# An encoder layer on one core: first loads of w_ff2 held behind a square, operands laid on or 64 bytes beside 128-byte multiples

## The chip, the cores and the metric

The kernel runs on one NeuronCore of a Trainium2 chip. The metric is the device time of one execution in microseconds. The kernel before took 1215.16 us, the median of 3 runs (1214.47, 1215.16 and 1220.26). The profile is of one further execution, which took 1215.97 us by the same clock.

Five engines are named as the profile names them: PE is TensorE's matmul, PEld its load of the stationary operand, DVE is VectorE, ACT is ScalarE, POOL is GpSimd, SP is SyncE. SP and POOL issue DMAs here.

## The reference

One encoder layer over 512 positions of 1024 channels, in float32:

```python
h = layer_norm(x, ln0_g, ln0_b)
proj = h @ w_in                       # q, k, v | z | x, B, C | dt | gates: 11328 columns
ya = neighbourhood_attention(q, k, v, rpb) @ w_attn_br
y  = ssd_chunked(silu(conv(x, B, C)), dt) in both directions, 8 groups
ys = rms_norm(y * silu(z)) @ w_ssd_br
h = layer_norm(ALPHA * h + (g0 * ya + g1 * ys) @ w_o)
out = layer_norm(ALPHA * h + square(relu(h @ w_ff1)) @ w_ff2)
```

`w_ff1` is 1024 x 4096 and `w_ff2` is 4096 x 1024.

## The kernel before, in words

**Three matmuls for one.** Each product is taken in float32r with operands split in a high and a low part. `mm3` (L351 to L354) issues three matmuls into one PSUM bank: stationary high with moving high (L352), stationary low with moving high (L353), stationary high with moving low (L354); the profile names a group as output, moving operand, stationary operand: in `ps_f<-wh_f,sqh` the weights move, in `ps_f<-h1Th,wh_f` they are stationary. Weights come from HBM as a float32 tile `ws_*` (1 MB, [128, 8, 256] or [128, 4, 512]), ACT copies it to the high part `wh_*`, and DVE or POOL subtracts to get the low part `wl_*`, each in two halves.

**Buffers.** The pool `wp` holds two buffers each of `ws`, `wh` and `wl`, 8192 bytes per partition. A matrix product therefore runs as a stream of "slabs": load, split, multiply, with the next slab's load waiting until a `ws` buffer is free. The pools `gc`, `sb`, `ge`, `rx0`, `fp`, `ffp` lie around `wp` in the order in which they are opened, from the left or from the right, so that the size of one shifts those behind it.

**Stages.** Up to about 512 us come the projections and the state-space branch, whose engine orders a planner class (`Plan`) writes out: group by group, `ps_x` (inputs x, B, C; 512 columns of `hT` moving, except group 0 with 256), `ps_z` (the slab `wh_z` is the moving operand, 256 columns, `hT` stationary), the scan, and `ps_sbr` (512 columns of `yT` moving). Then attention (to 716 us), its branch and gates, `ps_o` (256 columns of `wo` moving, `mgh`/`mgl` stationary), and the MLP from about 854 us.

**The MLP.** `ff1_tile(fq, f)` makes tile f (of 8) of quarter fq of the hidden layer: 24 matmuls of 512 columns into a bank `ps_f` (tag `mm`, two banks), then on ACT a Relu into `rl` (L1554), which frees the bank, and a Square into `r2` (L1560). The first four tiles of quarter 0 are taken in two halves of 256 columns, the first halves ahead of the second layer norm. Quarters 0 and 1 run first. Then `ff2_strassen` multiplies two quarters by `w_ff2` with seven block products. Its right operands are sums of two 512 x 512 blocks of `w_ff2`, made by DMA: `block` (L1448) loads one block of 1 MB from POOL's queue, and `plus` (L1454) adds the second in two DMAs of 512 KB that accumulate in SBUF. The tile is `w2r_*`: two of three lie in the pool `ffp` and one in `wp`'s `ws`. Its split writes `wh_f` on ACT (L1459) and `wl_f` on DVE (L1460). The left operands `sqh`, `sql` are tiles of tag `gt` in the pool `ge`, stationary.

**Order.** Past the planner's part the framework's scheduler sets each engine's order from the program and its dependencies; each engine and each DMA queue then runs strictly in that order. ACT therefore holds everything behind an instruction that waits.

Of the kernel before, what the change touches and what calls it, by code (L numbers as in the profile page):

```python
# [11 lines left out]
F32 = mybir.dt.float32  # L12
F32R = mybir.dt.float32r
# [6 lines left out]
P = 128  # L20
# [3 lines left out]
KD = D // P  # L24
# [9 lines left out]
OFF_Q, OFF_K, OFF_V, OFF_Z = 0, 1024, 2048, 3072  # L34
# [34 lines left out]
W0_ENG = lambda nc: (nc.gpsimd, nc.vector, nc.gpsimd, nc.vector)  # L69
# [3 lines left out]
class Plan:  # L73
# [16 lines left out]
                self.ap = self.make()  # L90
            return self.ap

    def tile(self, name, tag, pool, shape, dtype):
        return Plan.Tile(self, name, tag, lambda: pool.tile(shape, dtype, tag=tag, bufs=self.tags[tag],
                                                            name=name))

    def have(self, name, tag, ap):
        t = Plan.Tile(self, name, tag, None)
# [214 lines left out]
def encoder_layer(ctx, tc, x, w_in, w_attn_br, w_ssd_br, w_o, w_ff1, w_ff2, pcols, rows64,  # L313
                  d_skip, ln_rows, rpb_pad, consts, lmask, out, dbg=None):
    nc = tc.nc
# [6 lines left out]
    wp = ctx.enter_context(tc.tile_pool(name="wp", bufs=2))  # L322
# [20 lines left out]
                              op=ALU.subtract)  # L343
        return hi, lo

    def weights(parts, nk, ncol, name, eng=nc.vector, pool=None, after=None):
        hi = (pool or wp).tile([P, nk, ncol], F32R, tag="wh", name=f"wh_{name}")
        lo = (pool or wp).tile([P, nk, ncol], F32R, tag="wl", name=f"wl_{name}")
        return split_weights(parts, nk, ncol, name, hi, lo, eng, pool, after)

    def mm3(o, lh, ll, rh, rl, start, stop):  # L351
# [48 lines left out]
    gcp = gc.__enter__()  # L400
# [3 lines left out]
    gep = ge.__enter__()  # L404
# [2 lines left out]
    ident = cst[:, CC_ID : CC_ID + P]  # L407
    tri_f = cst[:, CC_TF : CC_TF + P]
    tri_b = cst[:, CC_TB : CC_TB + P]
    ones = gcp.tile([P, P], F32, name="ones")  # L410
    nc.vector.memset(ones, 1.0)
    eps = cp.tile([P, 1], F32, name="eps")
# [38 lines left out]
    def local(name, tag, shape, dtype=F32):  # L451
        return plan.tile(name, tag, sbp, shape, dtype)

    def slab(name, parts, nk, ncol, engs):

        ws = plan.tile(f"ws_{name}", "ws", wp, [P, nk, ncol], F32)
        wh = plan.tile(f"wh_{name}", "wh", wp, [P, nk, ncol], F32R)
        wl = plan.tile(f"wl_{name}", "wl", wp, [P, nk, ncol], F32R)
        c = 0
        keys = []  # L460
        for j, (src, r0, c0, n) in enumerate(parts):
            op("SP", 4.0 * n / ncol, lambda src=src, r0=r0, c0=c0, n=n, c=c: nc.sync.dma_start(
                ws()[:, :, c : c + n],
                src[r0 : r0 + nk * P, c0 : c0 + n].rearrange("(k p) c -> p k c", p=P)),
               r=[("behind", 0)], w=[(ws.name, j)], at=4.8 if name == "x0" else 4.4)
            keys.append((ws.name, j))
# [295 lines left out]

    def group_slabs(g):
        wb = slab(f"bc{g}", [(w_in, 0, OFF_B + g * P, P), (w_in, 0, OFF_C + g * P, P)], KD, 256,
                  (nc.gpsimd, nc.gpsimd) if g else W0_ENG(nc)[:2])
        wx = slab(f"x{g}", [(w_in, 0, OFF_X + g * 256, 256)], KD, 256,
                  (nc.gpsimd, nc.gpsimd) if g else W0_ENG(nc)[2:])
        return wb, wx

    def z_project(g):  # L770
        wh, wl = slab(f"z{g}", [(w_in, 0, OFF_Z + g * 256, 256)], KD, 256, (nc.gpsimd, nc.gpsimd))
        sz = local(f"sz{g}", "sz", [P, NT, 256])
        for c2 in range(2):
            ps = bank(f"ps_z{g}_{c2}", "mm", [P, 2, 256])
            for j in range(2):
                c = slice((2 * c2 + j) * P, (2 * c2 + j + 1) * P)
                for k in range(0, KD, 2):
                    def mms(k=k, j=j, c=c, ps=ps):
                        for q in (k, k + 1):
# [339 lines left out]
    for s in range(2):  # L1119
# [35 lines left out]
    for pr in range(NH // 2):  # L1155
# [25 lines left out]
        for hh in range(2):  # L1181
            h = 2 * pr + hh
# [91 lines left out]
    for k in range(KD):  # L1274
        ins = nc.scalar.activation(aTh[:, k], aT[:, k], AF.Copy)
# [95 lines left out]
    for t2 in range(2):  # L1371
        toks = (2 * t2, 2 * t2 + 1)
        for s in range(4):
            cs = slice(s * 256, (s + 1) * 256)
            wo = wos[s]
            tag = ("mm", "so")[s % 2]
            pss = {t: psx.tile([P, 256], F32, tag=tag, bufs=BANKS[tag], name=f"ps_o{t}_{s}")
                   for t in toks}
            for k in range(KD):
                for t in toks:  # L1380
                    ts_ = slice(t * P, (t + 1) * P)
                    mm3(pss[t], mgh[:, k, ts_], mgl[:, k, ts_], wo[0][:, k, :], wo[1][:, k, :],
                        k == 0, k == KD - 1)
            for t in toks:
                nc.vector.scalar_tensor_tensor(out=h0[t][:, cs], in0=h0[t][:, cs], scalar=ALPHA,
                                               in1=pss[t], op0=ALU.mult, op1=ALU.add)
        if t2:

            early = []
            for s in range(2):  # L1390
                w1 = weights([(w_ff1, 0, s * 256, 256)], KD, 256, f"f1_0_{s}")
                for j in range(2):
                    tag = ("so", "yd", "cb", "so")[2 * s + j]
                    ps = psx.tile([P, S], F32, tag=tag, bufs=BANKS[tag], name=f"ps_f1_0_{2 * s + j}")
                    ff1_half(w1, j, ps, 0)
                    early.append((w1, ps))
        for t in toks:
            layer_norm_core(epp, h0[t], acc[t], f"1_{t}")
        to_channels([acc[t] for t in toks], toks[0], 2, PC_G1, PC_B1, h1Th, h1Tl, epp, f"h1_{t2}")
# [5 lines left out]

    ffp = ctx.enter_context(tc.tile_pool(name="ffp", bufs=1, reuse_waits="tile"))
    NQ = D_FF // D
    pairs = [[gep.tile([P, 4, 256], F32R, tag="gt", bufs=4, name=f"sq{n}_{i}") for n in "hl"]
             for i in range(2)]
    turn = {"parts": 2, "raw": 0}  # L1410

    def parts(name, shape):

        turn["parts"] += 1
        if turn["parts"] % 3 == 0:
            return third(w3p, name, shape)
        return [wp.tile(shape, F32R, tag=n, name=f"{n}_{name}") for n in ("wh", "wl")]

    def raw(name):
        turn["raw"] += 1  # L1420
# [13 lines left out]
    def ff2_strassen(h, q0, r2):  # L1434
# [1 line left out]


        np_ = len(r2)
        begun, made = set(), [0]

        def rows(i, n, c, k=slice(0, 4)):
            r0 = q0 * D + (i * np_ + c) * 512
            return w_ff2[r0 : r0 + 512, n * 512 : (n + 1) * 512].rearrange(
                "(k p) c -> p k c", p=P)[:, k]

        def block(name, i, n, c):
            t = raw(f"{h}_{name}_{c}")
            nc.gpsimd.dma_start(t, rows(i, n, c))  # L1448
# [113 lines left out]
    slab = [None]  # L1562
# [5 lines left out]
    for fq in range(2):  # L1568
        for f in range(KD):
            ins = ff1_tile(fq, f, False)  # L1570
            if fq == 0 and f == 4:

                for t in range(NT):
                    for i, o in ((0, ALU.mult), (1, ALU.add)):
                        aff = nc.gpsimd.tensor_tensor(out=acc[t], in0=acc[t], in1=row1[i], op=o)
                        if t == 0 and i == 0:
                            tc.add_manual_dep(aff.ins, ins.ins.name, mybir.DependencyInfo(
                                mybir.DependencyClass.Sync, mybir.DependencyReason.DATA),
                                reason="behind the first channels")
# [107 lines left out]
```

## Time and profile before

| | us |
|---|---|
| median of 3 runs | 1215.16 |
| profiled execution, whole | 1215.97 |
| its span, first to last instruction | 1214.2 |
| PE busy | 1174.4 |
| DVE busy | 778.4 |
| ACT busy | 609.4 |
| POOL busy | 542.3 |

The span leaves out 1.8 us around the first and last instruction. PE's busy time is the union of its matmuls' times; a matmul's own duration in the profile runs from its issue to its modelled end and overlaps the next, so that what one matmul costs in a row of equal ones is the distance from its start to the next start, called its pace below. Where one stage has a long row of the same kind, the pace is read from the first and last start of one source line and its count.

### The profile page before, as it was taken

The page shows a single profiled execution, that of the slowest core. Times are in us where ns is not written, and L with a number is a line of the kernel's source. Part 1 is how long each engine was busy: PE and PEld are TensorE (multiplying, and loading weights), DVE is VectorE, ACT ScalarE, POOL GpSimd, SP SyncE. Part 2 cuts the span into 40 slices and gives each one's busy share as a digit, 9 for nine tenths or more (in the row PEclk, how much of TensorE's full clock was granted, in tenths as well). Part 3 has the DMA queues.
Part 4 walks back from the last instruction along what each step waited for, and adds up shares of the span by engine and source line. Part 5 has one row for each costly group of instructions (what it writes and reads, how often), then busy time and mean ns, then how long its engine had stood idle before and what let it go on. Part 6 is the DMA issues. An engine that isn't in the chain of part 4 may idle for free.

```text
span 1214.2 us, 16823 instructions
## 1 busy us (share of the span) xinstructions
PE 1174.4 (97%) x6306; PEld 1003.2 (83%) x6306; DVE 778.4 (64%) x1427; ACT 609.4 (50%) x1012; POOL 542.3 (45%) x588
## 2 busy tenths in 40 slices
PE   5999999999999999999999989999979999999996
PEld 5988798989888888788888878889968888878885
DVE  7748475665666665534888975356662467498856
ACT  4576573836355563324677873442254454365510
POOL 1158967777788767303666730014251131221000
PEclk9999999999999999999999999999999999999998
DMA  7144243333333342234432333353185586888511
GB/s 230 53 143 139 89 137 104 114 119 117 105 103 116 115 135 70 70 104 100 101 73 63 83 104 105 104 198 96 56 208 153 159 190 184 186 210 214 152 61 52
DMA packets 131169, 149.21 MB, mean 123 GB/s; under 512 B 22928, under 2 KB 105488, under 8 KB 131088
## 3 DMA queue, kind: packets, MB, share of 16 engines
q1 hardware_dynamic: 118032, 113.54, 30.5%
q0 software_dynamic: 13056, 34.61, 12.0%
q8 instruction: 49, 0.80, 0.3%
q14 instruction: 32, 0.26, 0.1%
HBM read 145.90 MB, written 2.23 MB: 122 GB/s over the span
## 4 chain that ended last, share of the span: by engine, by line
PE 80%; DVE 8%; DMA 4%; ACT 4%; issue 3%; POOL 0%; SPq 0%; DVEq 0%; POOLq 0%; ACTq 0%
PE ps_f L352 8%; PE ps_f L354 8%; PE ps_f L353 8%; PE ps_x L352 5%; PE ps_x L354 5%; PE ps_x L353 5%; PE ps_z L352 3%; PE ps_z L353 3%; PE ps_z L354 3%; PE yd L931 2%; PE ps_sbr L352 2%; PE ps_sbr L354 2%; PE ps_sbr L353 2%; DMA w2r<-in_w_ff 2%; PE ps_g L352 2%
## 5 line engine op out<-in xcount | busy, mean ns | idle before, releaser
L740 DVE SCALAR_TENSOR_TENSOR cv<-ps_x,pc,cv 128x511 f32<-128x511 f32 (+1 forms) x128 | 95.8, 749 | 26.0 <-ACT cv L732 22.2
L352 PE MATMUL ps_f<-h1Th,wh_f 128*128 128x512 f32 (+1 forms) x288 | 105.2, 369 | 5.9 <-ACT rl L1554 5.9
L353 PE MATMUL ps_f<-h1Th,wl_f 128*128 128x512 f32 (+1 forms) x288 | 105.4, 368 | 0.0
L354 PE MATMUL ps_f<-h1Tl,wh_f 128*128 128x512 f32 (+1 forms) x288 | 103.8, 369 | 1.1 <-DVE h1Tl L428 1.1
L1460 DVE TENSOR_TENSOR wl_f<-w2r,wh_f 128x1024 fp32r<-128x1024 f32 x42 | 49.7, 1222 | 63.0 <-ACT wh_f L1459 63.0
L352 PE MATMUL ps_z<-wh_z,hTh 128*128 128x256 f32 x256 | 76.0, 297 | 0.8 <-DVE cv L740 0.8
L354 PE MATMUL ps_z<-wl_z,hTh 128*128 128x256 f32 x256 | 72.4, 283 | 0.0
L353 PE MATMUL ps_z<-wh_z,hTl 128*128 128x256 f32 x256 | 72.3, 283 | 0.0
L352 PEld LDWEIGHTS ps_f<-h1Th,wh_f 128*128 128x128 f32 x288 | 54.7, 190 | 15.4 <-ACT rl L1554 6.4
L353 PE MATMUL ps_f<-wh_f,sql 128*128 128x512 f32 x168 | 66.3, 396 | 0.2 <-DVE sql L1460 0.2
L352 PE MATMUL ps_f<-wh_f,sqh 128*128 128x512 f32 x168 | 66.0, 396 | 0.4 <-ACT sqh L1459 0.4
L354 PE MATMUL ps_f<-wl_f,sqh 128*128 128x512 f32 x168 | 66.1, 395 | 0.0
L1448 POOL DMA_DIRECT2D w2r<-in_w_ff x18 | 15.2, 844 | 113.6 <-DVE wl_f L1460 74.0
L342 DVE TENSOR_TENSOR wl_f<-ws_f,wh_f 128x1024 fp32r<-128x1024 f32 x36 | 46.1, 1319 | 29.4 <-ACT wh_f L341 29.4
L1454 POOL DMA_DIRECT2D w2r<-in_w_ff x30 | 36.5, 1455 | 62.4 <-DMA w2r<-in_w_ff 38.8
L1047 DVE TENSOR_TENSOR ysacc<-ps_sbr,ysacc 128x512 f32<-128x512 f32 x56 | 38.4, 689 | 40.1 <-PE ps_sbr L354 39.7
L354 PEld LDWEIGHTS ps_f<-h1Tl,wh_f 128*128 128x128 f32 x288 | 53.7, 190 | 10.1 <-DVE h1Tl L428 1.3
L353 PEld LDWEIGHTS ps_f<-h1Th,wl_f 128*128 128x128 f32 x288 | 54.7, 190 | 8.9
L1319 POOL TENSOR_TENSOR gt<-gt,ysacc 128x512 f32<-128x512 f32 x8 | 12.8, 1602 | 105.1 <-ACT gt L1059 96.9
L341 ACT ACTIVATE wh_f<-ws_f 128x1024 fp32r<-128x1024 f32 x36 | 36.1, 1052 | 45.2 <-PE ps_o L353 22.1
L352 PE MATMUL ps_x<-hTh,wh_bc 128*128 128x512 f32 (+1 forms) x144 | 57.0, 396 | 1.6 <-ACT wh_bc L470 1.6
L1459 ACT ACTIVATE wh_f<-w2r 128x1024 fp32r<-128x1024 f32 x42 | 42.4, 1051 | 31.7 <-DMA w2r<-in_w_ff 19.2
(327 smaller groups left out, 3915.7 us busy)
## 6 DMA issues: line engine op xcount, KB each, us to landing
ws_f<-in_w_ff SPq DMA_DIRECT2D x20, 1024.0 KB
w2r<-in_w_ff POOLq DMA_DIRECT2D x18, 1024.0 KB, 5.6
bc<-acs_d SPq DMA_DIRECT2D x32, 512.0 KB
w2r<-in_w_ff POOLq DMA_DIRECT2D x30, 512.0 KB, 8.4
ws_bc<-in_w_in SPq DMA_DIRECT2D x16, 512.0 KB
ws_x<-in_w_in SPq DMA_DIRECT2D x8, 1024.0 KB
ws_z<-in_w_in SPq DMA_DIRECT2D x8, 1024.0 KB
ws_g<-in_w_in SPq DMA_DIRECT2D x8, 1024.0 KB
```

The costliest lines, as they stand in the source:

```text
L341: nc.scalar.activation(hi[:, k], st[:, k], AF.Copy)
L342: (eng[i] if isinstance(eng, tuple) else eng).tensor_tensor(out=lo[:, k], in0=st[:, k], in1=hi[:, k].bitcast(F32), op=ALU.subtract)
L352: nc.tensor.matmul(o, lh, rh, start=start, stop=False)
L353: nc.tensor.matmul(o, ll, rh, start=False, stop=False)
L354: nc.tensor.matmul(o, lh, rl, start=False, stop=stop)
L740: op("DVE", 0.75, lambda j=j, o=o, n=n: nc.vector.scalar_tensor_tensor(out=acc()[:, o], in0=ps()[:, n], scalar=tap(j), in1=acc()[:, o], op ...
L931: nc.tensor.matmul(yd()[:, c % 2, h * HD : (h + 1) * HD], bc()[:, 1, h, :], xtok()[:, c, h * HD : (h + 1) * HD], start=True, stop=True)
L1047: op("DVE", 0.69, lambda d=d, ps=ps: nc.vector.tensor_tensor(out=ysacc[:, d, :], in0=ps(), in1=ysacc[:, d, :], op=ALU.add), r=[(ps.name, 0 ...
L1448: nc.gpsimd.dma_start(t, rows(i, n, c))
L1454: nc.gpsimd.dma_start(t, rows(i, n, c, k), accum_op=ALU.add)
L1459: nc.scalar.activation(hi[:, k], x, AF.Copy)
L1460: nc.vector.tensor_tensor(out=lo[:, k], in0=x, in1=hi[:, k].bitcast(F32), op=ALU.subtract)
```

## The change

Four edits, all in where tiles lie, and one wait.

1. `wp`'s `wh` and `wl` buffers grow from 2048 to 2080 elements per partition. A slab takes 2048 of them through `wide(t, nk, shift)`, which starts `shift` elements in.
2. With `shift=16` (64 bytes) go the slabs that are used with 256 columns: all eight `z` slabs (moving operand), the `bc0` and `x0` slabs of group 0, and the two slabs `f1_0_0`, `f1_0_1` (stationary operands).
3. Three tiles that nothing uses, of 64, 32 and 96 bytes, are put into the pools `gc`, `rx0` and `ge`, so that what lies behind moves.
4. The first three block loads of the first Strassen pass must wait for `begin`, the Square of tile 0 of quarter 1.

```diff
+    def wide(t, nk, shift=0):
+        return t[:, shift : shift + 2048].rearrange("p (k c) -> p k c", k=nk)
...
-        wh = plan.tile(f"wh_{name}", "wh", wp, [P, nk, ncol], F32R)
-        wl = plan.tile(f"wl_{name}", "wl", wp, [P, nk, ncol], F32R)
+        wh, wl = [plan.tile(f"{n}_{name}", n, wp, [P, 2080], F32R, lambda t: wide(t, nk, shift))
+                  for n in ("wh", "wl")]
...
+    gcp.tile([P, 16], F32, name="gc_pad")
...
-        wh, wl = slab(f"z{g}", [(w_in, 0, OFF_Z + g * 256, 256)], KD, 256, (nc.gpsimd, nc.gpsimd))
+        wh, wl = slab(f"z{g}", [(w_in, 0, OFF_Z + g * 256, 256)], KD, 256, (nc.gpsimd, nc.gpsimd), 16)
...
+    rx0p.tile([P, 8], F32, name="rx_pad")
...
-                w1 = weights([(w_ff1, 0, s * 256, 256)], KD, 256, f"f1_0_{s}")
+                w1 = weights([(w_ff1, 0, s * 256, 256)], KD, 256, f"f1_0_{s}", shift=16)
...
+    gep.tile([P, 24], F32, name="ge_pad")
...
-            nc.gpsimd.dma_start(t, rows(i, n, c))
+            load = nc.gpsimd.dma_start(t, rows(i, n, c))
+            if fetched[0] < 3 and h == 0:
+                tc.add_manual_dep(load.ins, begin.ins.name, mybir.DependencyInfo(
+                    mybir.DependencyClass.Sync, mybir.DependencyReason.DATA),
+                    reason="behind the first quarter's squares")
+            fetched[0] += 1
...
+            if fq == 1 and f == 0:
+                begin = ins
```

**Where the operands lie.** Tile addresses in the two built programs, as the offset in a partition modulo 128 bytes; "next" is the stationary operand of the matmul that follows, which is loaded while this one runs.

| matmuls | count | moving, next stationary: before | after |
|---|---|---|---|
| 512 columns, `w2r` products (`sqh`, `sql` stationary) | 504 | 0, 96 | 0, 0 |
| 512 columns, `ps_sbr` (`yT` moving) | 384 | 64, 0 | 0, 0 |
| all other `mm3` matmuls of 512 columns | 2688 | 0, 0 | 0, 0 |
| 256 columns, `ps_z` | 768 | 0, 0 | 64, 0 |
| 256 columns, group 0's `ps_x` | 192 | 0, 0 | 0, 64 |
| 256 columns, halves of `ps_f1_0_0` to `_3` | 192 | 0, 0 | 0, 64 |
| 256 columns, `ps_dt` | 48 | 0, 64 | 0, 0 |
| 256 columns, `ps_o` | 384 | 0 or 64, 96 | 0 or 64, 96 |

A buffer of 8320 bytes is 65 times 128, so that after the change the second buffers of `wh` and `wl` lie 128 bytes past a multiple of 256. In 3450 places a 512-column `mm3` matmul is followed by another. Before, moving and next stationary operand lay at the same offset modulo 256 in 2587 of them (both at 0), and 32 or 64 bytes apart in the rest; after, 1718 are 0 apart modulo 256 and 1732 are 128 apart.

PE's order is the same row for row. POOL's, at the start of the MLP (`acc` are the residual rows, `row` the layer norm's affine rows, `w2r_3_0` is the block tile of product 3, part 0), before:

```order
L1575 TENSOR_TENSOR acc_7635<-acc_7635,row_7621 128x1024
L1448 DMA w2r_3_0_8925<-in_w_ff 128x4x512
L1448 DMA w2r_6_0_9010<-in_w_ff 128x4x512
L1575 TENSOR_TENSOR acc_7634<-acc_7634,row_7623 128x1024
L1575 TENSOR_TENSOR acc_7635<-acc_7635,row_7623 128x1024
L1454 DMA w2r_3_0_8925<-in_w_ff 128x2x512 x2
L1454 DMA w2r_6_0_9010<-in_w_ff 128x2x512 x2
L1575 TENSOR_TENSOR acc_7632<-acc_7632,row_7621 128x1024
L1575 TENSOR_TENSOR acc_7632<-acc_7632,row_7623 128x1024
L1448 DMA w2r_3_1_8963<-in_w_ff 128x4x512
L1454 DMA w2r_3_1_8963<-in_w_ff 128x2x512 x2
L1448 DMA w2r_6_1_9115<-in_w_ff 128x4x512
```

The same place on POOL after the change:

```order
L1595 TENSOR_TENSOR acc_7637<-acc_7637,row_7623 128x1024
L1595 TENSOR_TENSOR acc_7636<-acc_7636,row_7625 128x1024
L1595 TENSOR_TENSOR acc_7637<-acc_7637,row_7625 128x1024
L1595 TENSOR_TENSOR acc_7634<-acc_7634,row_7623 128x1024
L1595 TENSOR_TENSOR acc_7634<-acc_7634,row_7625 128x1024
L1461 DMA w2r_3_0_8928<-in_w_ff 128x4x512
L1461 DMA w2r_3_1_8966<-in_w_ff 128x4x512
L1461 DMA w2r_6_0_9013<-in_w_ff 128x4x512
L1472 DMA w2r_3_0_8928<-in_w_ff 128x2x512 x2
L1472 DMA w2r_3_1_8966<-in_w_ff 128x2x512 x2
L1472 DMA w2r_6_0_9013<-in_w_ff 128x2x512 x2
L1461 DMA w2r_6_1_9118<-in_w_ff 128x4x512
```

All eight additions of the affine rows now stand ahead of the loads, and the three loads stand together behind `begin`.

On ACT one row moves. At the end of quarter 0, before (`rl` is the Relu that frees a bank, `r` the Square, `wh_f_1_1` the slab of tiles 2 and 3 of quarter 1):

```order
L1554 ACTIVATE rl_5_8595<-ps_f_0_5_8570 128x512
L1560 ACTIVATE r_0_8416<-rl_5_8595 128x512
L341 ACTIVATE wh_f_1_1_8726<-ws_f_1_1_8728 128x1024 x2
L1459 ACTIVATE sqh_8414<-r_0_8416 128x512
L1554 ACTIVATE rl_6_8631<-ps_f_0_6_8606 128x512
```

The same place on ACT after the change:

```order
L1572 ACTIVATE rl_5_8598<-ps_f_0_5_8573 128x512
L341 ACTIVATE wh_f_1_1_8729<-ws_f_1_1_8731 128x1024 x2
L1578 ACTIVATE r_0_8419<-rl_5_8598 128x512
L1477 ACTIVATE sqh_8417<-r_0_8419 128x512
L1572 ACTIVATE rl_6_8634<-ps_f_0_6_8609 128x512
L1578 ACTIVATE r_0_8419<-rl_6_8634 128x512
L1572 ACTIVATE rl_7_8662<-ps_f_0_7_8637 128x512
```

The Square of tile 5 has gone behind the split; the Relu of tile 6 stands behind it in both. Further on, and in the same places before and after, stand the splits of the first block sums:

```order
L1572 ACTIVATE rl_3_8790<-ps_f_1_3_8765 128x512
L1477 ACTIVATE wh_f_0_3_0_8932<-w2r_3_0_8928 128x1024 x2
L1578 ACTIVATE r_1_8420<-rl_3_8790 128x512
L1572 ACTIVATE rl_4_8826<-ps_f_1_4_8801 128x512
L1578 ACTIVATE r_1_8420<-rl_4_8826 128x512
L1572 ACTIVATE rl_5_8854<-ps_f_1_5_8829 128x512
L1477 ACTIVATE wh_f_0_3_1_8970<-w2r_3_1_8966 128x1024 x2
```

So the Relus of tiles 4 and 5 of quarter 1 stand behind the arrival of `w2r_3_0`, and those of tiles 6 and 7 behind that of `w2r_3_1`.

More of the change, by code (lines that the diff above doesn't have):

```diff
@@ L91, in __call__, with tile @@
             return self.ap
-    def tile(self, name, tag, pool, shape, dtype):
-        return Plan.Tile(self, name, tag, lambda: pool.tile(shape, dtype, tag=tag, bufs=self.tags[tag],
-                                                            name=name))
+    def tile(self, name, tag, pool, shape, dtype, view=lambda t: t):
+        return Plan.Tile(self, name, tag, lambda: view(pool.tile(
+            shape, dtype, tag=tag, bufs=self.tags[tag], name=name)))
     def have(self, name, tag, ap):
@@ L344, in split_weights, with weights @@
         return hi, lo
-    def weights(parts, nk, ncol, name, eng=nc.vector, pool=None, after=None):
-        hi = (pool or wp).tile([P, nk, ncol], F32R, tag="wh", name=f"wh_{name}")
-        lo = (pool or wp).tile([P, nk, ncol], F32R, tag="wl", name=f"wl_{name}")
+    def wide(t, nk, shift=0):
+        return t[:, shift : shift + 2048].rearrange("p (k c) -> p k c", k=nk)
+    def weights(parts, nk, ncol, name, eng=nc.vector, pool=None, after=None, shift=0):
+        if pool:
+            hi, lo = [pool.tile([P, nk, ncol], F32R, tag=n, name=f"{n}_{name}") for n in ("wh", "wl")]
+        else:
+            hi, lo = [wide(wp.tile([P, 2080], F32R, tag=n, name=f"{n}_{name}"), nk, shift)
+                      for n in ("wh", "wl")]
         return split_weights(parts, nk, ncol, name, hi, lo, eng, pool, after)
@@ L452, in local, with slab @@
         return plan.tile(name, tag, sbp, shape, dtype)
-    def slab(name, parts, nk, ncol, engs):
+    def slab(name, parts, nk, ncol, engs, shift=0):
         ws = plan.tile(f"ws_{name}", "ws", wp, [P, nk, ncol], F32)
-        wh = plan.tile(f"wh_{name}", "wh", wp, [P, nk, ncol], F32R)
-        wl = plan.tile(f"wl_{name}", "wl", wp, [P, nk, ncol], F32R)
+        wh, wl = [plan.tile(f"{n}_{name}", n, wp, [P, 2080], F32R, lambda t: wide(t, nk, shift))
+                  for n in ("wh", "wl")]
         c = 0
@@ L764, in group_slabs @@
         wb = slab(f"bc{g}", [(w_in, 0, OFF_B + g * P, P), (w_in, 0, OFF_C + g * P, P)], KD, 256,
-                  (nc.gpsimd, nc.gpsimd) if g else W0_ENG(nc)[:2])
+                  (nc.gpsimd, nc.gpsimd) if g else W0_ENG(nc)[:2],
+                  0 if g else 16)
         wx = slab(f"x{g}", [(w_in, 0, OFF_X + g * 256, 256)], KD, 256,
-                  (nc.gpsimd, nc.gpsimd) if g else W0_ENG(nc)[2:])
+                  (nc.gpsimd, nc.gpsimd) if g else W0_ENG(nc)[2:],
+                  0 if g else 16)
         return wb, wx
     def z_project(g):
-        wh, wl = slab(f"z{g}", [(w_in, 0, OFF_Z + g * 256, 256)], KD, 256, (nc.gpsimd, nc.gpsimd))
+        wh, wl = slab(f"z{g}", [(w_in, 0, OFF_Z + g * 256, 256)], KD, 256, (nc.gpsimd, nc.gpsimd), 16)
         sz = local(f"sz{g}", "sz", [P, NT, 256])
@@ L1416, in parts @@
             return third(w3p, name, shape)
-        return [wp.tile(shape, F32R, tag=n, name=f"{n}_{name}") for n in ("wh", "wl")]
+        return [wide(wp.tile([P, 2080], F32R, tag=n, name=f"{n}_{name}"), shape[1])
+                for n in ("wh", "wl")]
     def raw(name):
@@ L1438, in ff2_strassen @@
         np_ = len(r2)
-        begun, made = set(), [0]
+        begun, made, fetched = set(), [0], [0]
         def rows(i, n, c, k=slice(0, 4)):
```

## The prediction, made before the change was run

> **What bounds the kernel now.** I read the page first, then the busy time by stage, then the chain of work that ended last, then the waits and the rows around the one place where the chain leaves PE for long.
>
> ```profile
> span 1214.2 us, 16823 instructions
> PE 1174.4 (97%) x6306; PEld 1003.2 (83%) x6306; DVE 778.4 (64%) x1427; ACT 609.4 (50%) x1012; POOL 542.3 (45%) x588
> ...
> PE 80%; DVE 8%; DMA 4%; ACT 4%; issue 3%; POOL 0%; SPq 0%; DVEq 0%; POOLq 0%; ACTq 0%
> ```
>
> PE is busy 97% of the span and is 80% of the chain. By stage (span of the stretch, then busy us and count of PE, PEld, DVE, ACT, POOL, then granted clock, DMA share, GB/s):
>
> ```profile
> 52.00:512.00 460.00, 456.02 (x2578) 391.88 (x2576) 282.51 (x473) 260.49 (x387) 337.69 (x348) 1.00 0.36 114
> 512.00:720.00 208.00, 203.65 (x1088) 173.16 (x1088) 151.03 (x413) 128.46 (x320) 101.65 (x165) 1.00 0.32 82
> 720.00:880.00 160.00, 158.96 (x984) 142.99 (x985) 96.45 (x171) 54.67 (x76) 31.11 (x14) 1.00 0.37 119
> 915.00:1065.00 150.00, 150.00 (x655) 122.47 (x654) 74.34 (x88) 66.70 (x88) 29.69 (x29) 1.00 0.70 173
> ```
>
> Outside the first 52 us PE idles 4 us in the state-space stage and nothing in the first Strassen pass; no other engine is busy over 75% there. So a nanosecond off each matmul's pace is time off the end, unless a chain through another engine has no more than that in hand. The exception lies between 880 and 915. Chain (start, us, engine, line) and waits of 895 to 915:
>
> ```profile
> 890.24 16.28 DMA ws_f<-in_w_ff
> 906.57 0.94 issue
> 907.50 1.04 ACT wh_f L341
> 909.60 0.80 PE ps_f L352
> ```
>
> ```profile
> ACT wh_f L341 <- DMA ws_f<-in_w_ff: 12.5, 1, 12.5
> ...
> PE ps_f L352 <- ACT rl L1554: 5.9, 1, 5.9
> ```
>
> ACT waits 12.5 us for slab `f1_1_1`, issued at 890.24. The Relu of tile 6 stands behind that split, so PE has no free bank for quarter 1's tile 0. The wait also costs clock (windows as above, then PE's timeline):
>
> ```profile
> 902.00:906.00 4.00, 1.65 (x8) 1.03 (x6) 0.00 (x0) 0.00 (x0) 0.00 (x0) 1.00 1.09 294
> 906.00:910.00 4.00, 0.40 (x1) 0.40 (x2) 2.37 (x3) 3.43 (x5) 0.00 (x0) 0.58 0.50 176
> 910.00:914.00 4.00, 4.00 (x11) 3.15 (x11) 2.92 (x4) 3.74 (x6) 0.00 (x0) 0.56 0.69 184
> ```
>
> ```profile
> 903.26 0.39 PE L354 MATMUL ps_f<-h1Tl,wh_f 128*128 128x512 f32 x1
> 909.60 0.80 PE L352 MATMUL ps_f<-h1Th,wh_f 128*128 128x512 f32 x1 [5.95 <-ACT rl L1554]
> ...
> 913.57 0.39 PE L352 MATMUL ps_f<-h1Th,wh_f 128*128 128x512 f32 x1
> ```
>
> The granted clock falls to 0.56 for some 5 us, and nine matmuls take 3.97 us.
>
> **The wait on `begin`.** What makes `f1_1_1` late? Queue shares of 890 to 904, then the same for 911.8 to 915.2, where one slab loads alone, and POOL's rows of the first sum:
>
> ```profile
> q0 software_dynamic: 1046, 2.04, 84.7%
> q1 hardware_dynamic: 719, 0.74, 19.7%
> ...
> q1 hardware_dynamic: 940, 0.95, 86.5%
> ```
>
> ```profile
> 881.37 1.81 POOL L1448 DMA_DIRECT2D w2r<-in_w_ff  x2
> ...
> 887.87 5.03 POOL L1454 DMA_DIRECT2D w2r<-in_w_ff  x4
> ```
>
> Between 890 and 904 the slabs' queue gets 0.74 MB in 14 us, beside 2.04 MB of accumulating loads; alone it moves 0.95 MB in 3.4 us. With the block loads held, `f1_1_1` should land about 5.5 us after issue (3.5 us of bytes at 0.28 MB/us and some 2 us before the first byte, from 910.02, the issue of that lone slab, to 911.8), near 896. ACT then splits by 898.1 (2 us), squares twice (1.3 us) and frees tile 6's bank near 900. PE needs it at 903.5. The stall goes, and so does the slow clock: 903.26 to 909.60 is 6.34 instead of 0.23, gain 6.1; 3.97 instead of 9 x 0.227 = 2.04, gain 1.9. Together 8.0 us. POOL's eight additions no longer have DMAs among them and end no later. What is late next on PE is nothing within 3 us.
>
> What the wait costs: `begin` is tile 0's Square, 5.45 us (24 x 0.227) and 1.2 us of ACT after 903.5, so 910.2. Then come three loads of 1 MB on POOL's queue, then six accumulating halves. Their rates (windows as above; landing times of the block loads of 860 to 960):
>
> ```profile
> 922.00:928.00 6.00, 6.00 (x28) 4.99 (x27) 2.36 (x2) 3.01 (x4) 0.21 (x1) 1.00 1.05 179
> ...
> 940.00:942.00 2.00, 2.00 (x11) 1.65 (x10) 0.00 (x0) 0.22 (x1) 0.00 (x0) 1.00 0.97 399
> DMA to landing us min/median/max: 5.2/6.9/15.1
> ```
>
> Plain block loads run at 399 GB/s (940 to 942), accumulating ones at 179 (922 to 928). The plain 3 MB end at 910.2 + 2 + 7.9 = 920.1; `w2r_3_0`'s 1 MB of accumulation at 926; at the shared 0.146 MB/us (2.04 MB in 14 us) at 927.3. ACT reaches its split after tile 3's Relu, 903.5 + 21.8 + 0.6 = 925.9, so it idles 0 to 2 us. PE is stopped only if tile 4's Relu ends after 936.2 (its bank is tile 6's), so the sum may land as late as 933. `w2r_3_1` lands 6 to 7 us on, 934 at worst, against 936.8; `w2r_6_0` at 941 against 947.7. By the medians nothing is on the path: cost 0. Upper end: three loads one behind the other at 5.2 us and the longest landing, 15.1, give 940.9; with 3.2 us of ACT behind it PE is 7.9 us late and the gain is given back. A gain is excluded, since no later work waits for these loads in the trace. I take 0, because the rates are the rows' own.
>
> **The layout.** Paces from first and last start in rows of equal matmuls (duration min/median/max, then starts). Two pairs, first the 512-column stretches 955 to 971.7, 478 to 487 and 971.8 to 982.6, then 256 columns, 51.6 to 63.3 and 807.9 to 837.9:
>
> ```profile
> L352 PE MATMUL ps_f<-wh_f,sqh x24: 393/395/397, 955.1 to 971.2; 128*128 128x512 f32 x24
> ...
> L354 PE MATMUL ps_sbr<-yTl,wh_sbr x12: 393/396/398, 478.9 to 486.6; 128*128 128x512 f32 x12
> ...
> L354 PE MATMUL ps_f<-h1Tl,wh_f x16: 389/389/396, 972.3 to 982.5; 128*128 128x512 f32 x16
> ```
>
> ```profile
> L353 PE MATMUL ps_z<-wh_z,hTl x32: 283/283/283, 51.9 to 63.1; 128*128 128x256 f32 x32
> ...
> L353 PE MATMUL ps_o<-wh_o,mgl x85: 277/280/285, 808.1 to 837.6; 128*128 128x256 f32 x85
> ```
>
> Every third matmul is of the line shown. 512 columns: 16.1 / (23 x 3) = 233.3 ns for offsets 0, 96; 7.7 / (11 x 3) = 233.3 for 64, 0; 10.2 / (15 x 3) = 226.7 for 0, 0. So either offset costs 6.6 ns. 256 columns is the other way: 11.2 / (31 x 3) = 120.4, read to 0.1 us (the constant 283 says an even pace; 120), for 0, 0, and 29.5 / (84 x 3) = 117.1 for `ps_o` at 96. Why 0, 0 should pay for 512 columns and lose for 256 the rows don't say; I use the numbers.
>
> - `w2r` products: 504 x 6.6 = 3.3 us. PE is busy all of 915 to 1065, so all of it counts.
> - `ps_sbr`: 384 x 6.6 = 2.5 us; `ps_z`: 768 x 2.9 = 2.2 us. For 256 columns at 64, 0 there is no row: the ends are 117.1 (the shifted row) and 120 (no effect). I take 117, since at 512 columns 64, 0 and 0, 96 are equal. Of these 4.7 us I count 85%, 4.0 us: the 4 us of PE idle show that other engines release PE in places, and some of what is saved is waited there.
> - Group 0 and the first halves of `f1_0`: 384 x 2.9 = 1.1 us; half lies ahead of waits on the first loads and the second layer norm, so 0.5. `ps_dt` loses 48 x 3 = 0.1.
> - 512 columns 128 bytes apart modulo 256 (1732 places): not in the trace. Nearest rows: 0 apart, 226.7; 32 and 64 apart, 233.3. So 0 to 11.4 us; below 0 excluded as far as the rows go, since no 512-column row is under 226.7. I take 0, the nearest row by place on a 128-byte grid: of offsets 0, 64 and 96 only the multiple of 128 is fast.
>
> The Trainium skill, "TensorE: Matmul & The Clock Gate", section "Step-by-step: what each phase is for", says that TensorE has two independent SBUF read ports, so that loading the next weights takes nothing from the running matmul. The rows at 233.3 and 226.7 differ by nothing but where the operands lie, so I give that rule little. By it the layout would be worth 0 and the sum 8 us.
>
> **Sum.** 8.0 + 3.3 + 4.0 + 0.5 - 0.1 = 15.7 us. The profiled execution took 1215.97, giving 1200.3; the median of the runs, 1215.16, lies 0.8 lower, giving 1199.5.
>
> **Rivals.**
>
> 1. *The grid is 256 bytes.* Then 1732 places run at 233.3 against 863 now: 869 x 6.6 = 5.7 us lost instead of 5.8 gained at 512 columns. 8.0 + 2.2 (the 256-column terms) - 5.7 = 4.5: 1210.7. For it: every fast row now lies on 256. Against it: nothing but the simpler grid.
> 2. *The layout is worth nothing*: the 6.6 ns belong to something else in those stages, or other engines take up all that PE saves. 1215.2 - 8.0 = 1207.2. Against: PE's busy share, and that the fast and slow rows alternate in one stage (955 to 971.7, 971.8 to 982.6). The rule of the Trainium skill on two ports, quoted above, would come out here.
> 3. *The block sums land late* and ACT, waiting in order for `w2r_3_0`, holds the Relus as it did for `f1_1_1`. From 933 each us is a us: 2 to 8 lost, 1201.5 to 1207.5. For it: 15.1 us is in the landing row, and slab `f1_2_0` loads in the same stretch.
> 4. *The other side: 128 apart is worse than 32 or 64.* At pace 226.7 + x the 1732 places cost 1.732 x us; from x = 9.1 ns (235.8) the whole gain is gone, from 12.6 (239.3) it is slower by over 0.5%. At 245 (x = 18.3) it would be 1215.2 - 15.7 + 31.7 = 1231. Against: of the rows of equal 512-column matmuls none is over 234.
>
> **How the numbers follow.** 0.5%, 6.1 us, is about what a measurement of this kernel tells from no change, so faster ends at 1209.1. Chances: forecast 0.68 (its own range 1197 to 1203, from the 85% and the half being anything); rival 1 0.14, a quarter of it under 1209.1; rival 2 0.05; rival 3 0.08; rival 4 0.05. Faster 0.68 + 0.05 + 0.08 + 0.03 = 0.84; same 0.11; slower 0.05. The range goes from 1197 to 1211, rival 1's place; it leaves out rival 4 and the forecast's low tail.
>
> **What would show it.** The wait of ACT for `ws_f` near 890 falls from 12.5 us to under 4, PE goes through 903 to 914 without a gap and with clock 1.00. `ps_f<-wh_f,sqh`, L353 `ps_sbr` fall from 395 to 389 ns a matmul, `ps_z` from 283 to about 280. ACT's wait for `w2r` near 926 stays under 7 us. I am wrong if groups that were at 389 (`ps_f<-h1Th,wh_f`) rise to 395 in slabs of the second buffers, or if PE waits for a Relu near 930.

## The result, and the profile after

The changed kernel took 1210.38 us (median of 17 runs, 1206.27 to 1217.19), the kernel before beside it 1216.41: ratio 0.9945, 95% interval 0.9931 to 0.9959, 6.0 us less. The prediction said 15.7 less. The time is inside the predicted range, at its upper end, where rival 1 (a grid of 256 bytes, 1210.7 us, chance 0.14) stood.

The profiled execution took 1212.09 us. First the page's head, PE's busy row and the shares of the chain:

```profile
span 1210.3 us, 16822 instructions
PE 1175.0 (97%) x6306; PEld 1001.2 (83%) x6306; DVE 776.4 (64%) x1427; ACT 609.2 (50%) x1012; POOL 543.2 (45%) x588
...
PE 82%; DVE 7%; ACT 3%; DMA 3%; issue 3%; POOL 1%; SPq 0%; DVEq 0%; POOLq 0%; ACTq 0%
```

PE is as busy as before (1174.4): what the change was to take off its matmuls is not gone. The wait, on the other hand, did what its part of the prediction said. Waits of 895 to 960 us, POOL's rows there, and the windows that held the gap:

```profile
ACT wh_f L1477 <- DMA w2r<-in_w_ff: 1.4, 1, 1.4
ACT wh_f L341 <- DMA ws_f<-in_w_ff: 0.8, 1, 0.8
```

```profile
914.29 2.55 POOL L1461 DMA_DIRECT2D w2r<-in_w_ff  x3 [11.98 <-ACT r L1578]
920.14 2.47 POOL L1472 DMA_DIRECT2D w2r<-in_w_ff  x2 [3.30 <-DMA w2r<-in_w_ff]
```

```profile
902.00:906.00 4.00, 4.00 (x19) 3.31 (x18) 2.00 (x2) 0.91 (x2) 0.32 (x1) 1.00 0.33 67
906.00:910.00 4.00, 4.00 (x19) 3.26 (x18) 1.30 (x2) 2.88 (x4) 0.00 (x0) 1.00 0.57 200
910.00:914.00 4.00, 4.00 (x19) 3.25 (x18) 1.66 (x2) 1.99 (x4) 0.00 (x0) 1.00 0.00 0
```

ACT's wait for the slab fell from 12.5 to 0.8 us, its wait for the block sum is 1.4 us, PE has no gap and the granted clock stays at 1.00. So the loss lies in the layout. Rows of equal matmuls (duration min/median/max, first and last start), in pairs of one slab in the first buffer and the next one in the second; then the `w2r` products, then `ps_z`:

```profile
L359 PE MATMUL ps_abr<-aTh,wh_abr x16: 389/389/393, 745.5 to 755.7; 128*128 128x512 f32 x16
...
L359 PE MATMUL ps_abr<-aTh,wh_abr x16: 390/393/404, 756.4 to 766.9; 128*128 128x512 f32 x16
```

```profile
L359 PE MATMUL ps_f<-h1Th,wh_f x16: 389/389/390, 896.0 to 906.2; 128*128 128x512 f32 x16
...
L359 PE MATMUL ps_f<-h1Th,wh_f x16: 390/393/404, 906.9 to 917.4; 128*128 128x512 f32 x16
...
L359 PE MATMUL ps_f<-wh_f,sqh x23: 387/392/404, 951.0 to 966.3; 128*128 128x512 f32 x23
```

```profile
L359 PE MATMUL ps_z<-wh_z,hTh x32: 279/279/284, 50.9 to 61.8; 128*128 128x256 f32 x32
```

One family of work, one stage, alternating with the buffer: 10.2 / (15 x 3) = 226.7 ns in the first buffer, 10.5 / 45 = 233.3 in the second, whose slabs stand 128 bytes off modulo 256 with a pitch of 2080 elements (8320 bytes, 32.5 times 256). That is the sign the prediction named for its failure. Mean ns from start to start over the whole trace, of the 3450 places whose starts lie under 270 ns apart (the rest hold a wait or slow clock), by the places of the moving and the next stationary operand modulo 256: 0, 0: 227.5 (1506 places); 128, 128: 227.7 (182); moving 0 and stationary 128: 232.6 (1518); moving 128 and stationary 0: 233.0 (152).

Matched matmul by matmul, the profiled execution after differs from the one before by (us): 512 columns, paces alone, +3.9 us (forecast -5.8 before the 85%); 512 columns, gaps and slow clock, -8.7; 256 columns, paces, -2.7; 256 columns, a new stall, +3.5. The last is this place, rows of PE, DVE and POOL:

```profile
119.25 0.35 PE L359 MATMUL ps_z<-wh_z,hTh 128*128 128x256 f32 x1 [1.88 <-DVE cv L748]
```

```profile
113.10 3.02 DVE L931 COPY_PREDICATED bc<-msk,bc 128x512 f32<-128x512 int32 x1
```

```profile
113.11 2.41 POOL L481 TENSOR_TENSOR wl_sbr<-ws_sbr,wh_sbr 128x1024 fp32r<-128x1024 f32 x1
```

and the same two of the kernel before:

```profile
113.94 0.76 DVE L921 COPY_PREDICATED bc<-msk,bc 128x512 f32<-128x512 int32 x1
```

```profile
113.95 2.99 POOL L473 TENSOR_TENSOR wl_sbr<-ws_sbr,wh_sbr 128x1024 fp32r<-128x1024 f32 x1
```

Both start within 0.01 us of each other. Before, the copy takes 0.76 us and POOL's subtraction 2.99, which ends 2.24 us behind the copy; after, the subtraction takes 2.41 and the copy 3.02, which ends 0.60 behind the subtraction. So it looks as if one ran at its own length and the other waited it out. The Trainium skill, "SBUF — State Buffer", section "SBUF: two separate sides", says that VectorE and GpSimd share a port pair as an exclusive lock, and that the one that comes second is blocked for the whole instruction; for VectorE this holds, among others, of an instruction with two inputs in SBUF, as the copy has, beside a GpSimd one that reads SBUF. The lengths agree with that; who comes first the rows don't show, since the copy's start stands 0.01 us ahead both times. The delay reached PE here (1.9 us of wait, and 1.5 of slow clock behind it, at a granted clock of 0.50 from 120.4 to 123 us). The stall is in the profiled executions of two kernels (this one and layout_only, below) and not in those of the other ones that left a usable trace; in how many of the runs without a profile it falls so isn't known.

### The profile page after: what moved, and what is told of

Read it like the earlier page. It is cut to its first block, busy times and chain, and to the rows that moved or that the text cites. A ratio compares the mean times of both kernels' runs of the same rounds, so it can differ in the third digit from the quotient of the medians.

```text
span 1210.3 us, 16822 instructions
## 1 busy us (share of the span) xinstructions
PE 1175.0 (97%) x6306; PEld 1001.2 (83%) x6306; DVE 776.4 (64%) x1427; ACT 609.2 (50%) x1012; POOL 543.2 (45%) x588
## 4 chain that ended last, share of the span: by engine, by line
PE 82%; DVE 7%; ACT 3%; DMA 3%; issue 3%; POOL 1%; SPq 0%; DVEq 0%; POOLq 0%; ACTq 0%
PE ps_f L361 8%; PE ps_f L359 8%; PE ps_f L360 8%; PE ps_x L361 5%; PE ps_x L359 5%; PE ps_x L360 5%; PE ps_z L359 2%; PE ps_z L360 2%; PE ps_z L361 2%; PE yd L941 2%; DMA w2r<-in_w_ff 2%; PE ps_sbr L359 2%; PE ps_sbr L361 2%; PE ps_sbr L360 2%; PE ps_g L359 2%
## 5 line engine op out<-in xcount | busy, mean ns | idle before, releaser
L359 PE MATMUL ps_sbr<-yTh,wh_sbr 128*128 128x512 f32 x128 | 55.8, 436 | 1.1 <-DVE ysacc L1057 0.6
```

The source lines that it names most:

```text
L359: nc.tensor.matmul(o, lh, rh, start=start, stop=False)
```

## The experiments

Theory A: a matmul's pace depends on the distance of its moving and its stationary operand modulo 256 bytes, so the change turned 863 slow places of 512 columns into 1,732. Theory B, the prediction's: multiples of 128 are all fast, and the missing 10 us went into stalls elsewhere. Theory C: the layout is worth nothing. Times are medians in us, each beside the kernel before on the same chip.

| kernel | time | before | ratio, 95% interval |
|---|---|---|---|
| changed kernel | 1210.38 | 1216.41 | 0.9945, 0.9931 to 0.9959 |
| wait_only | 1208.54 | 1217.21 | 0.9933, 0.9918 to 0.9947 |
| layout_only | 1218.20 | 1217.21 | 1.0012, 0.9998 to 1.0026 |
| grid0 | 1204.10 | 1217.21 | 0.9897, 0.9880 to 0.9915 |
| g256 | 1201.44 | 1217.21 | 0.9874, 0.9859 to 0.9890 |
| off128 | 1212.64 | 1218.41 | 0.9953, 0.9939 to 0.9968 |
| rel128 | 1203.77 | 1218.41 | 0.9882, 0.9855 to 0.9909 |
| late | 1201.86 | 1218.41 | 0.9864, 0.9840 to 0.9888 |
| sh192 | 1202.22 | 1218.41 | 0.9866, 0.9836 to 0.9896 |
| pitch | 1203.36 | 1219.03 | 0.9874, 0.9854 to 0.9895 |
| g256_2 | 1202.42 | 1219.03 | 0.9867, 0.9847 to 0.9888 |
| mixz | 1202.62 | 1219.03 | 0.9872, 0.9850 to 0.9893 |

One run of sh192, the profiled one, took 4167 us with PE busy for 99% of it; its trace is not used, and the median of the other four is 1202.09.

**The wait alone, the layout alone.** wait_only is the kernel before with the change's edit in `block` and `begin = ins` alone; layout_only is the changed kernel with the wait off:

```diff
-            if fetched[0] < 3 and h == 0:
+            if fetched[0] < 0 and h == 0:
```

> The kernel before with the wait on `begin` alone, no margin and no shift. All three theories leave the wait at what the trace of before priced: 8.0 us (6.1 of gap at 903.26 to 909.60, 1.9 of slow clock), so 1216.4 - 8.0 = 1208.4. Theory A (the pace of a matmul depends on moving operand and next stationary operand modulo 256 bytes) then needs the layout to cost 2 us in the changed kernel (1210.4). Theory B (a grid of 128 bytes, and new stalls elsewhere took 10 us) expects 1208.4 too, with the layout's gain lost in stalls. Theory C (the layout is worth nothing, and the changed kernel's whole 6.0 us are the wait, part of which is given back) expects the changed kernel's own time, 1210.4.

> The changed kernel without the wait: margins, shifts and pitch alone. A: 512-column places off the fast offset go from 863 to 1732, 869 x 6 ns = +5.2 us, and the 256-column families give back some 3 us, so 1216.4 + 2 = 1218.4. B: -7.7 us (the prediction's layout terms), 1208.7. C: 1216.4.

The wait alone is worth 8.7 us, the layout alone costs 1.0 (its interval takes in no change). wait_only is at A's and B's number; C's 1210.4 is just outside its spread. layout_only is 9.5 us over B's number and within 0.2 of A's: B falls. Beside its own kernel before it is 1.0 longer, where A had 2 longer and B 7.7 shorter. In layout_only's trace the old wait is back (waits of 890 to 925), with the new stall at 117 us beside it:

```profile
ACT wh_f L341 <- DMA ws_f<-in_w_ff: 12.7, 1, 12.7
...
PE ps_f L359 <- ACT rl L1572: 6.2, 1, 6.2
```

**All pairs 0 apart.** g256 repairs the layout (2112 also in `weights` and `parts`; `mx` and `sums` put 128 bytes more ahead of the squares); grid0 has the margins without pitch and shifts (slabs of `[P, 2048]`, `shift` 0, `ge_pad` 56 elements):

```diff
-        wh, wl = [plan.tile(f"{n}_{name}", n, wp, [P, 2080], F32R, lambda t: wide(t, nk, shift))
+        wh, wl = [plan.tile(f"{n}_{name}", n, wp, [P, 2112], F32R, lambda t: wide(t, nk, shift))
...
-            mx = atp.tile([P, 4], F32, tag="mx", bufs=2, name=f"mx{h}")
-            sums = atp.tile([P, 4], F32, tag="sums", bufs=2, name=f"sums{h}")
+            mx = gep.tile([P, 4], F32, tag="mx", bufs=2, name=f"mx{h}")
+            sums = gep.tile([P, 4], F32, tag="sums", bufs=2, name=f"sums{h}")
```

> The changed kernel with a pitch of 2112 instead of 2080 elements for the slabs and 56 instead of 24 elements ahead of the squares, so that all 512-column pairs of moving and next stationary operand are 0 apart modulo 256 bytes (1738 of 3588 are 128 apart in the changed kernel); shifts of 64 bytes for 256 columns stay (the row maxima and sums of the attention stage move into the margin ahead of the squares for room). A: 1738 x (232.7 - 227.0) = 9.9 us, of which 85 to 100% reach the end: 1210.4 - 8.4 to 9.9 = 1200.5 to 1202.0. B and C: nothing of the layout matters between the two, 1210.4.

> The kernel before with the wait, with the margins that bring yT and the squares to 0 modulo 256 bytes, and without pitch and shifts: all 3589 512-column pairs 0 apart, 256 columns nearly as in the kernel before. A and B: 8.0 + 863 x 6.6 ns x (85 to 100%) = 8.0 + 4.8 to 5.7, so 1202.7 to 1203.6. C: 1208.4 to 1210.4. Against g256 it prices the 64-byte shifts of 256-column slabs: A from the paces 119.6 to 114.3 and 117.7 of the changed kernel expects g256 2 to 3 us lower.

g256 came in at 1201.44, 15.8 us under the kernel before, and grid0 at 1204.10, 13.1 under it; A's numbers were 1200.5 to 1202.0 and 1202.7 to 1203.6. B and C had g256 at 1210.4, and C had grid0 at 1208.4 or more: C falls too. Matched matmul by matmul, g256 has 9.0 us less than the changed kernel in the paces of 512 columns (A: 9.9). The stall at 117 us is gone as well (3.5), and new waits between 512-column matmuls take as much back. Its stretch of 906 to 944 us, in which slabs of the first, second and third buffers follow each other:

```profile
L359 PE MATMUL ps_f<-h1Th,wh_f x55: 389/389/389, 905.8 to 942.5; 128*128 128x512 f32 x55
...
L359 PE MATMUL ps_f<-wh_f,sqh x3: 389/389/389, 943.2 to 944.6; 128*128 128x512 f32 x3
```

**Distance or place.** off128 and rel128 are grid0 with margins:

```diff
 off128
+    xpool.tile([P, 32], F32, name="hx_pad")        # ahead of hTh
 rel128
+    cp.tile([P, 32], F32, name="cp_pad")           # ahead of all slabs
-    gep.tile([P, 56], F32, name="ge_pad")
+    gep.tile([P, 24], F32, name="ge_pad")
```

> grid0 with one more margin of 128 bytes ahead of hTh, so that hT and h1T lie 128 bytes from the slabs: 2091 of 3589 512-column pairs are 128 apart modulo 256, 1900 of them with the moving operand at 128 (in the changed kernel nearly all had the next stationary one there). A: 2091 x 5.7 ns = +11.9 us over grid0's 1204.1; 256-column pairs at 0, 128 (857) have no row yet, between 0 and -4 us: 1212 to 1216. Theory B' (only a shifted stationary operand costs, or only the second buffers do): 191 x 5.7 = +1.1, 1205.

> grid0 with every operand of TensorE moved on by 128 bytes (a margin of 128 bytes ahead of all slabs, 128 less ahead of the squares): all 3589 512-column pairs at 128, 128. A in its relative form (what counts is the distance of the two modulo 256): 227 ns everywhere, 1204.1 as grid0. A in its absolute form (an operand that does not begin at a multiple of 256 costs): 3589 x 6 ns = +21 us, 1225.

off128 1212.64, rel128 1203.77: the distance counts, not the place. Matched with grid0, the paces of 512 columns are 9.4 us longer in off128 and 0.1 in rel128. The same gate products, all from one run of rows each, of off128 and of rel128:

```profile
L359 PE MATMUL ps_g<-hTh,wh_g x64: 390/393/404, 769.3 to 813.2; 128*128 128x512 f32 x64
```

```profile
L359 PE MATMUL ps_g<-hTh,wh_g x64: 389/389/389, 765.6 to 808.4; 128*128 128x512 f32 x64
```

43.9 / (63 x 3) = 232.3 against 42.8 / 189 = 226.5 ns. In off128 the 256-column pairs 128 apart ran at 118.6 to 119.0 ns, beside 119.7 at 0, 0: for these, 128 apart gains about 1 ns.

**The cost by itself.** A kernel of matmuls alone, one execution (`ds`, `dm`: shifts in bytes of stationary and moving operand; the layer is left out):

```python
for i in range(count):
    so = ds[i % len(ds)] // 4 + (i % 8) * P
    mo = dm[i % len(dm)] // 4 + (i % 3) * S
    nc.tensor.matmul(ps[:, 0:n], sta[:, so : so + P], mov[:, mo : mo + n], ...)
```

> The disputed cost by itself: the layer is left out, and only equal fp32r matmuls run, 48 of 512 columns or 96 of 256 columns into one bank for each placing, with nothing beside them. `c512sta32x` is 512 columns with the stationary operands 32 bytes on and the moving ones at 0, `c512mov32x` the reverse, `own` alternates stationary 0, d against moving d, 0 (a matmul's two operands differ, its moving operand and the next stationary agree), `next` alternates 0, d against 0, d (its own agree, the next differs), `both` has both at d. A (distance modulo 256): 512 columns 227 ns at 0, 256 and in `both`, 233 at every other placing, 128 included, for `sta` and `mov` alike. B (grid of 128): 227 at 128 too. If the load of the next weights meets the running stream, `next` is slow and `own` fast; if the matmul's own pair counts, the reverse; both slow if either does. 256 columns after the changed kernel's rows: 120 at 0 and 128, 114 at 64 and 192 and 117 at 32 and 224 for `sta`, 118 for `mov64`. Rival: the pace depends on the traffic of other engines, not on the places: one pace for all placings.

```profile
L87 PE MATMUL ps_c512sta0x<-mov,sta x48: 389/389/397, 24.0 to 34.6; 128*128 128x512 f32 x48
...
L87 PE MATMUL ps_c512sta128x<-mov,sta x48: 390/393/404, 68.5 to 79.4; 128*128 128x512 f32 x48
...
L87 PE MATMUL ps_c512sta256x<-mov,sta x48: 389/389/390, 113.0 to 123.7; 128*128 128x512 f32 x48
...
L87 PE MATMUL ps_c512both128x<-mov,sta x48: 389/389/396, 257.4 to 268.0; 128*128 128x512 f32 x48
...
L87 PE MATMUL ps_c256mov64x<-mov,sta x96: 279/279/283, 393.7 to 404.9; 128*128 128x256 f32 x96
...
L87 PE MATMUL ps_c256mov192x<-mov,sta x96: 276/276/286, 439.2 to 450.0; 128*128 128x256 f32 x96
```

Mean ns from start to start, from the trace's starts:

| bytes | 0 | 32 | 64 | 96 | 128 | 160 | 192 | 224 | 256 |
|---|---|---|---|---|---|---|---|---|---|
| 512 columns, stationary shifted | 226.7 | 233.2 | 233.4 | 234.2 | 232.5 | 233.4 | 229.0 | 233.3 | 226.7 |
| 512 columns, moving shifted | | 233.4 | 229.1 | 233.6 | 233.4 | 234.1 | 233.2 | 233.1 | |
| 256 columns, stationary shifted | 120.0 | 118.3 | 117.8 | 117.3 | 120.0 | 119.9 | 117.8 | 117.8 | 119.9 |
| 256 columns, moving shifted | | 117.8 | 117.8 | 119.9 | 118.7 | 117.4 | 113.7 | 118.3 | |

Both shifted alike: 226.7 (64) and 226.9 (128) at 512 columns, 120.0 at 256. With next to nothing beside it on the core (ACT and DVE are busy for 5% of the span each, POOL for 0.2 us), A's table of 512 columns stands, 128 included, but for one case: with the stationary operand 64 bytes behind the moving one (stationary at 192 or moving at 64) it is 229, not 233. The rival, other engines' traffic, is out. Which stationary operand meets the stream isn't one of the two: with 128 bytes between a matmul's own operands, but none to the next stationary one, 230.0; the other way round 228.4. Each costs a part. Why the distance costs anything no run shows. 256 columns follow no rule that the table shows, except that equal places are among the slowest and 64 apart gains 2 ns or more; A's 114 for the stationary operand at 64 and 192 failed, both took 117.8.

**How much per place, and the 256 columns again.** pitch is the changed kernel with 2112 in place of 2080 and nothing else; mixz is g256 with 48 instead of 16 elements in `z_project`'s slabs; sh192 has 48 in all shifted slabs.

> The changed kernel with one number changed: the slabs' pitch 2112 instead of 2080 elements, so that second buffers too lie at multiples of 256 bytes; the squares stay at 128. 504 of 3588 512-column pairs (the w2r products) are 128 apart, against 1738. A: (1738 - 504) x 5.7 ns = 7.0 us, 85 to 100% of it at the end: 1203.4 to 1204.5 against the changed kernel's 1210.4, and 2 to 3 over g256. B (128 apart costs nothing; the 10 us went into stalls that g256's other places happened to avoid): no fixed number, 1210.4 if the stalls stay.

> g256 once more, as the partner of the two others on one chip: 1201.4.

> g256 with the `ps_z` slabs shifted by 192 bytes instead of 64, the others still by 64. In the run of matmuls alone, 256 columns with the moving operand at 192 and the stationary one at 0 took 113.7 ns, with 64 at 0 117.8. If that holds in the layer, ps_z falls from 118 to 114, 768 x 4 = 3.1 us, 85% of it at the end: 2.6 us under g256_2, 1198.8. If the layer's other traffic sets that pace: level with g256_2.

> g256 with shifts of 192 instead of 64 bytes for the 256-column slabs. 512-column pairs stay 0, 0. In the changed kernel 256-column pairs at (moving 0, next stationary 64) and (0, 192) ran at 114 to 115 ns, (64, 0) at 117.7, and 0, 0 at 119.6. If the distance alone counts, (192, 0) is the mirror of (0, 64): `ps_z` falls from 118 to about 114, 768 x 3.5 = 2.7 us, of which 85%: 1199.1. If a shifted moving operand costs its own few ns, `ps_z` stays at 118 and the time at 1201.4.

pitch, one number in three places, takes the changed kernel from ratio 0.9945 to 0.9874; A's 1203.4 to 1204.5 came out as 1203.36. That is partly luck: by the ratios the step is 8.6 us where A had 6.0 to 7.0. Matched with the changed kernel, pitch has 5.8 us less in the paces of 512 columns, and 3.0 come from the stall at 117 us, which its trace doesn't have and A had not counted. g256_2, which also mends the 504 `w2r` products, is only 0.9 us under pitch where A said 2 to 3, which is less than either spreads over its runs. The paces do fall (3.1 us, matched), and PE then waits ahead of the next block product. The end of tile 7's first-layer work and the product behind it, PE's rows of pitch and of g256, and g256's waits of 1035 to 1060:

```profile
1053.30 0.40 PE L361 MATMUL ps_f<-h1Tl,wh_f 128*128 128x512 f32 x1
1053.53 0.40 PE L359 MATMUL ps_f<-wh_f,sqh 128*128 128x512 f32 x1
```

```profile
1051.91 0.39 PE L361 MATMUL ps_f<-h1Tl,wh_f 128*128 128x512 f32 x1
1054.27 0.50 PE L359 MATMUL ps_f<-wh_f,sqh 128*128 128x512 f32 x1 [1.98 <-ACT sqh L1477]
```

```profile
ACT wh_f L1477 <- DMA w2r<-in_w_ff: 13.3, 2, 7.4
```

In pitch 0.23 us lies between them, in g256 2.36 (the granted clock stays at 1.00): ACT makes `sqh` late because it stood 13.3 us at splits of blocks that had not landed, 10.2 in pitch. By these waits the block sums' DMAs are the next bound there, at about 1202 us; no run tests it. mixz and sh192 stay level with g256 (1202.62 against 1202.42; 1202.22): moving `ps_z` to 192 bytes, 113.7 ns in the run of matmuls alone, gave 116.4 instead of 117.2 ns in the layer (mixz against g256_2). The expectation of 2.6 us failed; the lone number did not carry over.

**The wait later.** late is g256 with `begin` at tile 2 of quarter 1 (`if fq == 1 and f == 2`; the expectation's "quarter 0" is a slip).

> g256 with the loads waiting for the Square of quarter 0's tile 2 instead of tile 0, two tiles or 10.9 us later; nothing left out. In g256 the second half of the first block sum landed at 925.05, 1.9 us after ACT asked for it, and PE did not stop. Rival 3's mechanism: the sum lands near 936, split and Relu end near 937.7, PE needs that bank at 932.4: 5.3 us of gap and 1 to 2 of slow clock behind it, 1201.4 + 6 to 7 = 1207.5 to 1208.5. The other theory (a landing later than the Relus' order can take up is hidden elsewhere): 1201.4.

1201.86, level with g256. This does not refute rival 3, since the scheduler had moved ACT's work too. ACT's rows of late show the Relus of 927.68 and 933.12 ahead of the split, while g256 split after the one of 921.63:

```profile
927.68 0.60 ACT L1572 ACTIVATE rl<-ps_f 128x512 f32<-128x512 f32 x1 [4.18 <-PE ps_f L361]
928.31 0.63 ACT L1578 ACTIVATE r<-rl 128x512 f32<-128x512 f32 x1
933.12 0.60 ACT L1572 ACTIVATE rl<-ps_f 128x512 f32<-128x512 f32 x1 [4.18 <-PE ps_f L361]
933.61 1.05 ACT L1477 ACTIVATE wh_f<-w2r 128x1024 fp32r<-128x1024 f32 x1
```

What a late landing costs with ACT's order as it was in the changed kernel stays open; that order was not held fixed in any run.

## Why the prediction was wrong, point by point

- *The failed step*: "512 columns 128 bytes apart modulo 256 (1732 places): ... I take 0, the nearest row by place on a 128-byte grid." The term measured 9.0 us, the matched difference between the changed kernel and g256 in the paces of 512 columns: 5.2 ns a place (the run of matmuls alone has 232.5 - 226.7 = 5.8). It lay within the bounds that the prediction gave (0 to 11.4), but the value taken was the wrong end. All fast rows of before were at distance 0, which fits a grid of 128, of 256 or of anything larger; the choice of 128 rested on no row. The nearest rows in bytes, 32 and 64 apart, were slow and pointed to the other end. With 9.0 in it the sum would have been 15.7 - 9.0 = 6.7 us, 1208.5 from 1215.16. So this one term makes 9.0 of the 9.7 us that were missing (15.7 - 6.0). That the time still fell inside the range is due to rival 1, whose place set the range's upper end.
- *The wait*, 8.0 us: right, 8.7 in wait_only's runs, with the gap (6.1) gone in its trace and nothing late behind it. Slab `f1_1_1` came as forecast, issued at 892.05 and split from 897.62, 5.6 us for 5.5. Of the two parts of that 5.5, the 2 us before the first byte was misread: the lone slab's packets begin at 911.06, not 911.8, and last 4.1 us. "By the medians nothing is on the path: cost 0": ACT waited 1.4 us for the block sum where 0 to 2 was forecast, and PE did not stop.
- *The `w2r` products*, 3.3, and *`ps_sbr`*, 2.5: the mechanism was right and the places were wrong. In the changed kernel they gained 1.1 and 0.3 in pace, since slabs or squares were still 128 apart; in g256, where they are 0 apart, 3.2 and 1.5. All other 512-column work, whose places 128 apart stood in the sum with 0, lost 5.2 us in the changed kernel.
- *256 columns*: `ps_z` 2.2 forecast, 1.4 measured (279 ns a matmul and some 117.7 of pace, where 117 was taken); group 0 and `f1_0` 0.5 forecast, 1.8 of pace measured, at 114 to 115 ns, faster than any row of before. `ps_o`, moved by the margins without a term in the sum, lost 0.5.
- *"Of these 4.7 us I count 85%"*: the profile shows both cases. grid0 to g256, 3.8 us of 256-column pace, came out as 2.7 in the medians; the last 3.1 us of `w2r` pace came out as 0.9. The new stall of 3.5 us at 117 us was not foreseen.
- *Rival 1* had the count and the direction right, and 256 as the number; by rel128 it is a distance modulo 256 and not a grid. That its 1210.7 lies so near 1210.38 is partly luck: its gain was 4.5 us and 6.0 was measured, and the kernel before took 1216.41 beside the changed one, not 1215.16. Its chance, 0.14, was too low: all that stood against it was "nothing but the simpler grid", which is no row.
- *Rival 2*, the Trainium skill's rule in "TensorE: Matmul & The Clock Gate", section "Step-by-step: what each phase is for" (two independent read ports, so a weight load takes nothing from the running matmul): the run of matmuls alone shows 226.7 and 232.5 ns with nothing but 128 bytes between them. The measurement decides against the rule at that size, 2.6%. The load of the next weights need not be the whole of it: in that run the distance to the next stationary operand alone cost 1.7 ns, the one between a matmul's own operands 3.3.
- *The forecast's number* was reachable: g256, with 1201.44 and 1202.42, is 15.8 and 16.6 us under its kernels before, and pitch 15.7. That g256 meets 15.7 so closely is in part chance: matched, it has 5.2 us in the paces of 512 columns (forecast 5.4 after the 85%) and 4.0 in those of 256 (2.3), and other waits give some of it back.

## What to carry to other kernels

When all fast cases of a profile share one value, the next multiple down is a guess, not a row: price an unseen place by both neighbours, and test it by itself before a buffer pitch depends on it. Here, lay the moving and the stationary operand of long fp32r matmuls at the same offset modulo 256 bytes, the second buffer included (a pitch that is a multiple of 256), which was worth 2.6% of their pace. And once PE is the bound, look for where the saved time stops: at 1202 us the waits already point at the block sums' DMAs.

## What the runs showed of the hardware

- 512-column fp32r matmuls, 128 x 128 stationary: 226.7 ns at equal places modulo 256 bytes, 229 to 234 at all other shifts in steps of 32, with next to no other work on the core. The distance counts, not the place (rel128: 3345 of the 3450 places, all at 128, 128, have a mean of 227.4, the rest wait or run at a slow clock).
- 256 columns go the other way: 120.0 ns at equal places, 113.7 to 120.0 elsewhere, and not the same in the layer as alone (moving at 192: 113.7 alone, 116.4 in mixz).
- A COPY_PREDICATED on DVE and a subtraction on POOL that start 0.01 us apart fell either way: 0.76 and 2.99 us before, 3.02 and 2.41 after.
